# A seven-product Strassen scheme for the second MLP's down projection in a two-layer trunk

## The chip, the cores and the metric

The kernel runs on one core of one Trainium2 chip. Its time is the time of one execution in device microseconds (us), taken as the median of three runs, lower being better. Before the change it is 1189.18 us (1189.01 to 1190.25). The profile shows one execution of its own, taken by the hardware profiler; this document reads it by engine: PE (TensorE, matmuls), PEld (its loads of the stationary operand), DVE (VectorE), ACT (ScalarE), POOL (GpSimd) and SP (SyncE, which here only issues DMAs).

## The reference, cut to what matters

The trunk has two layers on 512 tokens of width 1024: a sparse-attention mixer with its MLP, then a convolution mixer with its MLP, and a last norm. The change lies in the second MLP, which is the last thing before that norm:

```python
def sq_relu_mlp(h, w1, w2):
    return jnp.square(jax.nn.relu(h @ w1)) @ w2

h = h + y
h = h + sq_relu_mlp(rmsnorm(h, norm_mlp_g[i]), mlp_w1[i], mlp_w2[i])
return rmsnorm(h, final_g)
```

`w1` is 1024 x 4096 and `w2` is 4096 x 1024, all in float32. Everything is computed to nearly float32 precision.

## The kernel before

**Three matmuls per product.** The engine multiplies numbers in a shorter float32 format (`F32R`). So each float32 operand is taken apart into a rounded part (hi) and a rest (lo), and a product is three matmuls: hi with hi, hi with lo, lo with hi (`mm3`, L90). For a weight this is `split` (L81): ACT copies the raw weight into `whi` (L86), then DVE subtracts to give `wlo` (L87). A unit of `split` here is 128 x 512 numbers, and units live in a ring of 12 buffers (`wsplit_mid`). Raw weights come as loads of 1 MB each, issued by SP, into a ring of two buffers (`wraw`).

**The second MLP** works in four groups g of 1024 hidden columns. In each group the up projection makes eight blocks j of hidden columns: 24 matmuls of 128 x 512 into a PSUM bank, then `hidden` inside `up_proj`: DVE does relu and the token scale (`hr`, L636), ACT squares it twice (`hf` in float32 at L638, `hh` as hi at L641), DVE subtracts for `hl` (L642). So each block has one trip from DVE to ACT and back. The first two blocks of group 0 (`ahead`) are computed early, at the end of the convolution's stage.

**The down projection** (L986 to L1014) takes each half of the 1024 output columns in turn. Four PSUM banks `dps`, one for each block b of 128 tokens, collect 8 k x 3 matmuls; the stationary operand is a 128 x 128 piece of `hh` or `hl`, the moving one a 128 x 512 weight unit. DVE then adds the bank to the result `y[b]` in SBUF (L1010). `y` starts as the transposed residual: 32 small transposes on PE into `rt` banks (L957) which ACT copies out (L958). In the last group `squares` and `finish` do the last norm (one `pow` on POOL for each block, L183) and store. The last half of the last group goes block by block of tokens, so that only one block's norm and store are left after the last matmul.

**Order.** A scheduler that simulates a timeline lays out each engine's queue when the program is built; at run time every engine goes through its own queue in order and waits on semaphores.

Of the kernel before, what the change touches and what calls it, by code (L numbers as in the profile page):

```python
# [18 lines left out]
P = 128  # L19
S = 512  # L20
D = 1024
KC = D // P
NB = S // P
# [19 lines left out]

ROW = 512
FILL = 64


@with_exitstack
def kernel(
# [7 lines left out]
    nc = tc.nc  # L57
# [42 lines left out]
    def bank(name="mm"):  # L100
        return acc.tile([P, S], F32, tag="mm", name=name)
# [57 lines left out]
    hT = [resid.tile([P, S], F32, name=f"hT{c}") for c in range(KC)]  # L159
# [469 lines left out]
    def up_proj(w, rr, pool, st=None, block=None, ahead=()):  # L629

        block = block or proj(w, g2)
        hid = []

        def hidden(ps):
            r = pool.tile([P, S], F32, tag="hr", name="hr", bufs=2)
            nc.vector.scalar_tensor_tensor(r, ps, 0.0, rr[0], op0=OP.max, op1=OP.mult)  # L636
            f = pool.tile([P, S], F32, tag="hf", name="hf", bufs=2)
            nc.scalar.activation(f, r, AF.Square)  # L638
            th = pool.tile([P, S], F32R, tag="hh", name="hh", bufs=10)
            tl = pool.tile([P, S], F32R, tag="hl", name="hl", bufs=10)  # L640
            nc.scalar.activation(th, r, AF.Square)  # L641
            nc.vector.tensor_sub(tl, f, th.bitcast(F32))  # L642
            hid.append((th, tl))

        done = 0
        if st is not None:
            first = list(ahead) or block([0])
            cols = rms_cols(st)
            first += block([1]) if len(first) < 2 else []
            rr[:] = [broadcast(cols, NB, bank("bc"))]  # L650
            for ps in first:
                hidden(ps)
            done = 2
        for j in range(done, KC):
            hidden(block([j])[0])
        return hid
# [11 lines left out]
            if k == 0:  # L668
                pw1.extend(ps)

    wsplit.append(ctx.enter_context(tc.tile_pool(name="wsplit_mid", bufs=12)))
    conv_ctx = ExitStack()
    late = conv_ctx.enter_context(tc.tile_pool(name="late", bufs=1))
    diags = [late.tile([P, max(TAPS0[c][0], TAPS1.get(c, (0, 0))[0]), 4, 32], F32, name=f"diag{c}")
# [53 lines left out]
            table(AF.Sigmoid, ghi[KC - 1].bitcast(F32))  # L728


    HS = S // 2
# [208 lines left out]
    conv_ctx.close()  # L940


    with tc.tile_pool(name="m2", bufs=1) as m2, \
            tc.tile_pool(name="m2_ps", bufs=2, space=PSUM) as m2_ps:
        fg = m2.tile([P, D], F32, name="fg")
        nc.scalar.dma_start(fg, final_g.rearrange("(o d) -> o d", o=1).to_broadcast([P, D]))
        y = [m2.tile([P, D], F32, name=f"y{b}") for b in range(NB)]
        ysq = small.tile([P, NB, 2], F32, name="ysq")
        fo = {}

        def residual():
            for b in range(NB):
                for half in range(2):
                    ps = m2_ps.tile([P, S], F32, tag="misc", name="rt")
                    for z in range(4):
                        c = 4 * half + z
                        nc.tensor.transpose(ps[:, z * P:(z + 1) * P], hT[c][:, b * P:(b + 1) * P], ident)  # L957
                    nc.scalar.activation(y[b][:, half * S:(half + 1) * S], ps, AF.Copy)  # L958

        def squares(b, half):  # L960

            hs = slice(half * S, (half + 1) * S)
            sq = tmp.tile([P, S], F32, tag="sq", name="sq")
            nc.scalar.activation(sq, y[b][:, hs], AF.Square, accum_out=ysq[:, b, half:half + 1])
            o = m2.tile([P, S], F32, tag=f"fo{half}", name="fo", bufs=3) if half else y[b][:, hs]
            nc.vector.tensor_mul(o, y[b][:, hs], fg[:, hs])
            fo[b, half] = o

        def finish(b):
            s1 = small.tile([P, 1], F32, tag="fs", name="fs", bufs=2)  # L970
            nc.vector.tensor_add(s1, ysq[:, b, 0:1], ysq[:, b, 1:2])
            r1 = inv_root(s1, 1, 1.0 / D, f"fr{b}")
            for half, eng in ((0, nc.sync), (1, nc.scalar)):
                o = fo[b, half]
                if half:
                    nc.vector.tensor_scalar(o, o, r1, None, op0=OP.mult)
                else:
                    nc.scalar.activation(o, o, AF.Copy, scale=r1)
                eng.dma_start(out[0, b * P:(b + 1) * P, half * S:(half + 1) * S], o)

        rr = []
        for g in range(NG):
            hid = up_proj(mlp_w1[1][:, g * D:(g + 1) * D], rr, m2, *((st, up, ahead) if g == 0 else ()))
            if g == 0:
                residual()
            w2 = mlp_w2[1][g * D:(g + 1) * D, :]  # L986
            for half in range(2):
                hs = slice(half * S, (half + 1) * S)
                last = g == NG - 1 and half == 1
                dps = [bank(f"dps{b}") for b in range(NB)]  # L990

                def mms(b, k, u):
                    tb = slice(b * P, (b + 1) * P)
                    mm3(dps[b], hid[k][0][:, tb], hid[k][1][:, tb], u[0][:, 0, :], u[1][:, 0, :],
                        k == 0, k == KC - 1)

                for k0 in (0, 4):
                    raw = load(w2, k0, 4, half * S, S)
                    units = []
                    for z in range(4):  # L1000
                        u = split(raw[:, z:z + 1, :])
                        units.append(u)
                        if not (last and k0):
                            for b in range(NB):
                                mms(b, k0 + z, u)
                for b in range(NB):
                    if last:
                        for z in range(4):
                            mms(b, 4 + z, units[z])
                    nc.vector.tensor_add(y[b][:, hs], dps[b], y[b][:, hs])  # L1010
                    if g == NG - 1:
                        squares(b, half)
                    if last:
                        finish(b)  # L1014


# [22 lines left out]
```

## Time and profile before

| What | us |
|---|---|
| Median of three runs | 1189.18 |
| The profiled execution's own time | 1186.75 |
| Its span (first to last instruction) | 1185.0 |
| PE busy in the span | 1150.8 |
| DVE busy | 663.3 |
| ACT busy | 498.2 |
| First matmul of the second MLP's first down projection | 873.1 |
| Last matmul of the program starts | 1177.75 |

A group of rows by line names the engine, the operation, the tiles written and read, the shape, the count, then the busy time in us and the mean of one in ns; behind the second bar stands how long the engine sat idle just before these instructions and who ended that. A row of a timeline gives start and duration in us; "x3" means three instructions merged, with the duration from the first start to the last end. Ends of matmuls are modelled, so how fast matmuls follow each other is read from their starts.

### The profile page before, as it was taken

The page shows a single profiled execution, that of the slowest core. Times are in us where ns is not written, and L with a number is a line of the kernel's source. Part 1 is how long each engine was busy: PE and PEld are TensorE (multiplying, and loading weights), DVE is VectorE, ACT ScalarE, POOL GpSimd, SP SyncE. Part 2 cuts the span into 40 slices and gives each one's busy share as a digit, 9 for nine tenths or more (in the row PEclk, how much of TensorE's full clock was granted, in tenths as well). Part 3 has the DMA queues.
Part 4 walks back from the last instruction along what each step waited for, and adds up shares of the span by engine and source line. Part 5 has one row for each costly group of instructions (what it writes and reads, how often), then busy time and mean ns, then how long its engine had stood idle before and what let it go on. Part 6 is the DMA issues. An engine that isn't in the chain of part 4 may idle for free.

```text
span 1185.0 us, 15284 instructions
## 1 busy us (share of the span) xinstructions
PE 1150.8 (97%) x5828; PEld 948.5 (80%) x5828; DVE 663.3 (56%) x1195; ACT 498.2 (42%) x936; POOL 247.5 (21%) x248
## 2 busy tenths in 40 slices
PE   7999999999999999999999988899999999999997
PEld 6778888877888888888888666689888888888886
DVE  4589854476434434434444998878544434434434
ACT  5353454545423423423435544466632432432422
POOL 2436643322005000000012667632100000000000
PEclk8999999999999999999999998999999999999999
DMA  6122222215233323322323563533322332332211
GB/s 229 36 71 72 89 84 77 71 36 182 78 100 107 98 80 107 107 83 78 125 71 116 151 172 91 161 108 115 117 86 92 107 107 72 106 107 92 86 36 71
DMA packets 104353, 117.84 MB, mean 99 GB/s; under 512 B 3817, under 2 KB 87609, under 8 KB 104280
## 3 DMA queue, kind: packets, MB, share of 16 engines
q1 hardware_dynamic: 102440, 112.89, 30.6%
q10 hardware_dynamic: 1840, 3.97, 0.9%
q8 instruction: 46, 0.75, 0.3%
q14 instruction: 27, 0.22, 0.1%
HBM read 112.56 MB, written 4.29 MB: 99 GB/s over the span
## 4 chain that ended last, share of the span: by engine, by line
PE 81%; DVE 12%; DMA 2%; issue 2%; ACT 1%; POOL 1%; SPq 0%; POOLq 0%; DVEq 0%; ACTq 0%
PE mm L91 19%; PE mm L93 19%; PE mm L92 19%; PE dps L93 5%; PE dps L92 5%; PE dps L91 5%; DVE score L482 2%; DVE m L480 2%; DVE conv L802 2%; DVE wlo L87 2%; DVE pa L798 1%; PE vps L91 1%; PE vps L92 1%; PE vps L93 1%; DMA xs<-in_x_dram 1%
## 5 line engine op out<-in xcount | busy, mean ns | idle before, releaser
L86 ACT ACTIVATE whi<-wraw 128x512 fp32r<-128x512 f32 x378 | 234.6, 631 | 469.9 <-PE mm L92 317.1
L92 PE MATMUL mm<-glo,whi 128*128 128x512 f32 (+1 forms) x928 | 337.0, 365 | 1.2 <-DVE glo L175 1.2
L93 PE MATMUL mm<-ghi,wlo 128*128 128x512 f32 (+1 forms) x928 | 337.1, 365 | 0.0
L91 PE MATMUL mm<-ghi,whi 128*128 128x512 f32 (+1 forms) x928 | 334.6, 366 | 1.9 <-ACT whi L86 0.8
L87 DVE TENSOR_TENSOR wlo<-wraw,whi 128x512 fp32r<-128x512 f32 x325 | 233.5, 726 | 177.7 <-ACT whi L86 174.1
L92 PEld LDWEIGHTS mm<-glo,whi 128*128 128x128 f32 x928 | 175.0, 189 | 31.0 <-issue 2.4
L91 PEld LDWEIGHTS mm<-ghi,whi 128*128 128x128 f32 x928 | 173.1, 189 | 32.6 <-issue 2.8
L93 PEld LDWEIGHTS mm<-ghi,wlo 128*128 128x128 f32 x928 | 175.0, 189 | 28.7 <-issue 1.1
L93 PE MATMUL mm<-hh,wlo 128*128 128x512 f32 x256 | 99.6, 389 | 0.0
L92 PE MATMUL mm<-hl,whi 128*128 128x512 f32 x256 | 99.6, 389 | 0.0
L92 PE MATMUL dps<-wlo,hh 128*128 128x512 f32 x256 | 99.6, 389 | 0.0
L91 PE MATMUL mm<-hh,whi 128*128 128x512 f32 x256 | 99.1, 389 | 0.0
L91 PE MATMUL dps<-whi,hh 128*128 128x512 f32 x256 | 99.1, 389 | 0.0
L93 PE MATMUL dps<-whi,hl 128*128 128x512 f32 x256 | 98.6, 389 | 0.0
L636 DVE SCALAR_TENSOR_TENSOR hr<-mm,rmsb 128x512 f32<-128x512 f32 x64 | 44.1, 691 | 91.9 <-PE mm L93 90.2
L87 POOL TENSOR_TENSOR wlo<-wraw,whi 128x512 fp32r<-128x512 f32 x53 | 70.9, 1342 | 89.6 <-ACT whi L86 89.5
L183 POOL TENSOR_TENSOR fr<-v,mhalf 128x1 f32<-128x1 f32 x4 | 2.2, 548 | 340.2 <-DVE v L181 340.2
L642 DVE TENSOR_TENSOR hl<-hf,hh 128x512 fp32r<-128x512 f32 x64 | 44.6, 697 | 41.9 <-ACT hh L641 41.9
L206 POOL TENSOR_TENSOR ss<-sq 128x512 f32<-128x512 f32 (+1 forms) x4 | 5.7, 1434 | 270.3 <-ACT sq L201 270.3
L790 POOL TENSOR_TENSOR pa<-pa,pt 128x512 f32<-128x512 f32 (+1 forms) x43 | 53.6, 1249 | 32.6 <-ACT pt L788 30.5
L92 PEld LDWEIGHTS mm<-hl,whi 128*128 128x128 f32 x256 | 48.0, 188 | 10.1
L92 PEld LDWEIGHTS dps<-wlo,hh 128*128 128x128 f32 x256 | 48.0, 188 | 10.0
(257 smaller groups left out, 1588.2 us busy)
## 6 DMA issues: line engine op xcount, KB each, us to landing
wraw<-in_mlp_w_dram SPq DMA_DIRECT2D x64, 1024.0 KB, 5.2
wraw<-in_conv_w_pw_dram SPq DMA_DIRECT2D x12, 1024.0 KB
wraw<-in_dsa_w_in_dram SPq DMA_DIRECT2D x10, 1024.0 KB, 9.1
wraw<-in_dsa_w_out_dram SPq DMA_DIRECT2D x4, 1024.0 KB, 4.9
sh<-flat SPq DMA_DIRECT2D x12, 260.0 KB, 3.6
sh<-flat SPq DMA_DIRECT2D x20, 138.0 KB, 2.8
xw<-in_dsa_w_in_dram ACTq DMA_DIRECT2D x4, 584.0 KB, 7.4
xs<-in_x_dram SPq DMA_DIRECT2D x4, 512.0 KB, 12.1
```

What stands on the lines that cost most here:

```text
L86: nc.scalar.activation(hi, src, AF.Copy)
L87: (eng or nc.vector).tensor_sub(lo, src, hi.bitcast(F32))
L91: nc.tensor.matmul(ps, wh, xh, start=start, stop=False)
L92: nc.tensor.matmul(ps, wh, xl, start=False, stop=False)
L93: nc.tensor.matmul(ps, wl, xh, start=False, stop=stop)
L480: nc.vector.max(m8s[-1], score[i])
L482: nc.vector.match_replace(score[i], m8s[i - 1], score[i], TAKEN)
L636: nc.vector.scalar_tensor_tensor(r, ps, 0.0, rr[0], op0=OP.max, op1=OP.mult)
L642: nc.vector.tensor_sub(tl, f, th.bitcast(F32))
L790: nc.gpsimd.tensor_add(pa, pa, pt)
L798: nc.vector.scalar_tensor_tensor(pa, sh(t), wt(t), pa, op0=OP.mult, op1=OP.add)
L802: nc.vector.scalar_tensor_tensor(cps, sh(t), wt(t), cps, op0=OP.mult, op1=OP.add)
```

## The change

The down projection of the second MLP is written anew. In a group, the 1024 hidden columns (k) are taken as even and odd blocks, the 512 tokens as two halves and the output columns as two halves. That is a 2 x 2 by 2 x 2 block product, which needs eight products of blocks when multiplied out; the new code forms seven (`p1`, `q5`, `q6`, `p2`, `p7`, `p3`, `p4`) from sums of blocks of weights and sums of blocks of hidden values. A product is 4 k x 2 token blocks x 3 = 24 matmuls of 128 x 512. Running sums stay in PSUM: `al` collects p1, q6, p7 and p4 in turn, `ga` q5 and p3, `be` p2. After each product DVE adds the two banks to two blocks of `y`, or subtracts them.

What else changes with it (line numbers of the kernel after):

- `hidden` (L1009) makes, for each pair of blocks j, seven operands of 256 tokens, in hi and lo: `b11`, `d1` from the even block, `b21`, `b22`, `e2`, `e3`, `e4` from the odd one. Sums go into the storage of `hT`, which is free by then. A pair has two trips from DVE to ACT and back in each block.
- Sums of weights (L1067, L1070, L1071, L1081) are DVE instructions of 128 x 2048, four in a group.
- The ring of split units has 8 buffers (`wsplit_m2`) in the place of 12, in storage of its own that opens when the old ring closes.
- The `rt` transposes stand ahead of the stage and have four PSUM banks; PE's order through the stage is the order of the code.
- In the last group two blocks of tokens end together in place of one.

```diff
-            w2 = mlp_w2[1][g * D:(g + 1) * D, :]
-            for half in range(2):
-                dps = [bank(f"dps{b}") for b in range(NB)]
...
-                for k0 in (0, 4):
-                    raw = load(w2, k0, 4, half * S, S)
...
-                    nc.vector.tensor_add(y[b][:, hs], dps[b], y[b][:, hs])
+        def parts(src, hi, lo):
+            nc.scalar.activation(hi, src, AF.Copy)
+            nc.vector.tensor_sub(lo, src, hi.bitcast(F32))
+
+        def hidden(j, ps):
...
+            nc.vector.scalar_tensor_tensor(r, ps, 0.0, rr[0], op0=OP.max, op1=OP.mult)
...
+                nc.scalar.activation(v[:, 0:3:2], r, AF.Square)
+                nc.vector.tensor_sub(v[:, 1], v[:, 0], v[:, 2])
+                parts(v[:, :2], xs[0][i], xs[1][i])
...
+                nc.scalar.activation(u[:, :2], r, AF.Square)
+                nc.vector.scalar_tensor_tensor(u[:, 2], u[:, 1], -1.0, v[:, 1], op0=OP.mult, op1=OP.subtract)
+                nc.vector.tensor_sub(u[:, 3], u[:, 1], v[:, 2])
+                nc.vector.scalar_tensor_tensor(u[:, 4], u[:, 2], -1.0, u[:, 0], op0=OP.mult, op1=OP.subtract)
+                parts(u, xs[2][i], xs[3][i])
+            a = {"a11": raw(0, 0), "a21": raw(1, 0), "a22": raw(1, 1, "wd")}
+            def product(bk, name, wn, xn, start):
+                for k in range(4):
+                    hi, lo = split(a[wn][:, k:k + 1, :])
+                    xh, xl = xop[xn, k]
+                    for z in range(2):
...
+                        for n, (l, m) in enumerate(((xh, hi), (xl, hi), (xh, lo))):
+                            nc.tensor.matmul(banks[bk, z], l[:, zs], m[:, 0, :], start=start and k == n == 0,
...
+            product("al", "p1", "a11", "b11", True)
+            to("al", 0, 0, OP.add)
+            s = a["s"] = m2.tile([P, 4, S], F32, tag="wd", name="ws", bufs=2)
+            nc.vector.tensor_add(s, a["a21"], a["a22"])
+            product("ga", "q5", "s", "d1", True)
+            to("ga", 1, 1, OP.subtract)
+            nc.vector.tensor_add(s, s, a["a11"])
+            nc.vector.tensor_add(a["a21"], a["a21"], a["a11"])
+            a["a12"] = raw(0, 1)
+            product("al", "q6", "s", "e2", False)
+            to("al", 1, 0, OP.add)
+            product("be", "p2", "a12", "b21", True)
...
+            product("al", "p7", "a21", "e3", False)
...
+            nc.vector.tensor_add(s, s, a["a12"])
+            product("ga", "p3", "s", "b22", False)
...
+            product("al", "p4", "a22", "e4", False)
```

Where the queues change. Until the last matmuls of the convolution's stage every engine has the same instructions in the same order and with the same waits as before. The first place is PE at the start of the stage: `rt` are the transposes of the residual, `bc` spreads the token scale over the partitions, `mm<-ghi` is the up projection's block j = 2. Before:

```order
L957 MATMUL rt<-ident,hT_102 128x128
L957 MATMUL rt<-ident,hT_103 128x128
L191 MATMUL bc<-diag,ones 128x128
L91 MATMUL mm<-ghi_104,whi 128x512
L92 MATMUL mm<-glo_112,whi 128x512
```

Now:

```order
L217 MATMUL rms_ps<-ones,ss 128x1 x2
L964 MATMUL rt<-ident,hT 128x128 x12
L193 MATMUL bc<-diag,ones 128x128 x2
L964 MATMUL rt<-ident,hT 128x128 x4
L193 MATMUL bc<-diag,ones 128x128 x2
L92 MATMUL mm<-ghi_97,whi 128x512
L93 MATMUL mm<-glo_105,whi 128x512
```

All transposes and all four `bc` now stand ahead of block j = 2; before, three `bc` and eight transposes came after it or in it. The second place is DVE in the up projection of a group, from the `hr` of one block to those that follow. Before:

```order
L636 SCALAR_TENSOR_TENSOR hr<-mm,rmsb 128x512
L87 TENSOR_TENSOR wlo<-wraw,whi 128x512
L642 TENSOR_TENSOR hl<-hf,hh 128x512
L87 TENSOR_TENSOR wlo<-wraw,whi 128x512
L636 SCALAR_TENSOR_TENSOR hr<-mm,rmsb 128x512
```

Now (`hT` is the borrowed storage for the sums, `xl` the lo parts, `ws` the sum of two raw weights):

```order
L88 TENSOR_TENSOR wlo<-wraw,whi 128x512
L1025 SCALAR_TENSOR_TENSOR hT<-hT 128x256
L1026 TENSOR_TENSOR hT<-hT 128x256
L1027 SCALAR_TENSOR_TENSOR hT<-hT 128x256
L88 TENSOR_TENSOR wlo<-wraw,whi 128x512
L1007 TENSOR_TENSOR xl_7750<-hT,xh_7746 128x1280
L1015 SCALAR_TENSOR_TENSOR hr<-mm,rmsb 128x512
L1067 TENSOR_TENSOR ws<-wraw 128x2048
L88 TENSOR_TENSOR wlo<-wraw,whi 128x512
L1020 TENSOR_TENSOR hT<-hT 128x256
L88 TENSOR_TENSOR wlo<-wraw,whi 128x512
L1071 TENSOR_TENSOR wraw<-wraw 128x2048
```

Sums that the down projection needs (L1067, L1071) now stand in DVE's queue inside the up projection, behind the `hr` of block 4 and ahead of that of block 5. The third place is SP's queue of loads for one group; `128x8x256` is a raw piece of `w1`, `128x4x512` one of `w2`:

```order
L77 DMA wraw<-in_mlp_w_dram 128x8x256 x2
L1034 DMA wraw<-in_mlp_w_dram 128x4x512
L77 DMA wraw<-in_mlp_w_dram 128x8x256 x2
L1034 DMA wraw<-in_mlp_w_dram 128x4x512 x3
L77 DMA wraw<-in_mlp_w_dram 128x8x256 x2
```

Eight loads of 1 MB for a group, as before, but one of `w2` (`a22`, into a buffer of its own) now goes ahead of the last two of `w1`; of the three that follow these, the first is `a11`, the second `a21`, the third `a12`.

## Rows read from the trace of the kernel before

**Rows 1.** The page's busy times, then its 40 slices of the span for PE, and for the granted clock of PE.

```profile
PE 1150.8 (97%) x5828; PEld 948.5 (80%) x5828; DVE 663.3 (56%) x1195; ACT 498.2 (42%) x936; POOL 247.5 (21%) x248
...
PE   7999999999999999999999988899999999999997
...
PEclk8999999999999999999999998999999999999999
```

**Rows 2.** Busy times by stage: the stretch, its length, then busy us of PE, PEld, DVE, ACT and POOL, the granted clock, the DMA engines' share and GB/s. The up projection of group 1, its down projection, and the whole from the first down projection's start to the last matmul.

```profile
916.60:960.20 43.60, 43.60 (x194) 36.09 (x193) 21.53 (x33) 18.23 (x30) 0.00 (x0) 1.00 0.29 97
960.20:1003.80 43.60, 43.60 (x194) 36.12 (x193) 15.71 (x24) 11.30 (x18) 0.00 (x0) 1.00 0.30 97
...
873.10:1178.00 304.90, 304.90 (x1346) 252.25 (x1344) 126.76 (x197) 99.27 (x167) 1.63 (x3) 1.00 0.26 86
```

**Rows 3.** All instructions on the tile `dps`: duration in ns (least, median, most), and the first and last start; the load of a stationary operand, its matmul, and the last matmul of the three.

```profile
L91 PEld LDWEIGHTS dps<-whi,hh x256: 187/188/188, 873.1 to 1177.1; 128*128 128x128 f32 x128
L91 PE MATMUL dps<-whi,hh x256: 389/389/389, 873.3 to 1177.3; 128*128 128x512 f32 x128
...
L93 PE MATMUL dps<-whi,hl x256: 388/389/389, 873.8 to 1177.7; 128*128 128x512 f32 x128
```

**Rows 4.** Groups of DVE's instructions from 850 us to the end, shapes kept apart.

```profile
L87 DVE TENSOR_TENSOR wlo<-wraw,whi 128x512 fp32r<-128x512 f32 x110 | 75.8, 689 | 93.6 <-ACT whi L86 93.6
L1010 DVE TENSOR_TENSOR y<-dps,y 128x512 f32<-128x512 f32 x32 | 20.9, 688 | 31.0 <-PE dps L93 31.0
L642 DVE TENSOR_TENSOR hl<-hf,hh 128x512 fp32r<-128x512 f32 x30 | 20.8, 693 | 20.5 <-ACT hh L641 20.5
L636 DVE SCALAR_TENSOR_TENSOR hr<-mm,rmsb 128x512 f32<-128x512 f32 x29 | 20.1, 692 | 44.9 <-PE mm L93 44.9
```

**Rows 5.** The same for the whole span, DVE's shapes of 256 elements and one row from a time when POOL is busy.

```profile
L860 DVE TENSOR_TENSOR u<-u,dr 128x256 f32<-128x256 f32 x16 | 6.7, 418 | 0.6 <-ACT dr L847 0.6
...
L900 DVE SCALAR_TENSOR_TENSOR hT<-mm,pv,hT 128x256 f32<-128x256 f32 x12 | 5.5, 479 | 6.2 <-PE mm L93 6.2
...
L817 DVE TENSOR_TENSOR u<-u,pilot 128x512 f32<-128x512 f32 x1 | 1.6, 1649 | 0.0
```

**Rows 6.** DVE in order of time: three instructions one behind the other, for the lo parts and for the adds to `y`.

```profile
818.96 1.89 DVE L87 TENSOR_TENSOR wlo<-wraw,whi 128x512 fp32r<-128x512 f32 x3
...
1154.37 2.05 DVE L1010 TENSOR_TENSOR y<-dps,y 128x512 f32<-128x512 f32 x3 [7.48 <-PE dps L93]
```

**Rows 7.** Groups of ACT's instructions, the first three from 850 us to the end, the last of the whole span.

```profile
L86 ACT ACTIVATE whi<-wraw 128x512 fp32r<-128x512 f32 x109 | 69.1, 634 | 183.4 <-PE dps L93 103.1 <-PE mm L92 77.2 <-ACT hh L641 2.0
L638 ACT ACTIVATE hf<-hr 128x512 f32<-128x512 f32 x29 | 18.4, 635 | 10.2 <-DVE hr L636 10.2
L641 ACT ACTIVATE hh<-hr 128x512 fp32r<-128x512 f32 x29 | 17.8, 615 | 0.0
...
L858 ACT ACTIVATE ghi<-u 128x256 fp32r<-128x256 f32 x16 | 6.7, 416 | 0.4
```

**Rows 8.** The start of the second MLP in order of time, on PE, POOL and DVE.

```profile
836.00 0.50 PE L215 MATMUL rms_ps<-ones,ss 128*128 128x1 f32 x4
...
836.78 1.53 POOL L183 TENSOR_TENSOR rms<-v,mhalf 128x4 f32<-128x4 f32 x1 [3.89 <-DVE v L181]
...
838.35 0.87 DVE L190 TENSOR_SCALAR diag<-ident,rms 128x128 f32<-128x128 f32 x4 [0.91 <-POOL rms L183]
...
838.93 0.47 PE L91 MATMUL mm<-ghi,whi 128*128 128x512 f32 x1
...
842.46 0.83 PE L191 MATMUL bc<-diag,ones 128*128 128x128 f32 x6
843.05 0.48 PE L91 MATMUL mm<-ghi,whi 128*128 128x512 f32 x1
...
845.22 1.03 PE L957 MATMUL rt<-ident,hT 128*128 128x128 f32 x8
846.01 0.47 PE L91 MATMUL mm<-ghi,whi 128*128 128x512 f32 x1
```

**Rows 9.** DMA issues by line: count, KB each, median us from issue to landing; the MLP's weights, and the four first loads of the program, which go out together.

```profile
wraw<-in_mlp_w_dram SPq DMA_DIRECT2D x64, 1024.0 KB, 5.2
...
xs<-in_x_dram SPq DMA_DIRECT2D x4, 512.0 KB, 12.1
```

**Rows 10.** The end of the program in order of time.

```profile
1177.75 0.39 PE L93 MATMUL dps<-whi,hl 128*128 128x512 f32 x1
...
1178.17 0.69 DVE L1010 TENSOR_TENSOR y<-dps,y 128x512 f32<-128x512 f32 x1 [0.78 <-PE dps L93]
...
1180.20 0.55 POOL L183 TENSOR_TENSOR fr<-v,mhalf 128x1 f32<-128x1 f32 x1 [2.18 <-DVE v L181]
1180.78 0.72 ACT L978 ACTIVATE y<-y,fr 128x512 f32<-128x512 f32 x1 [1.09 <-POOL fr L183]
```

More of the change, by code (lines that the diff above doesn't have):

```diff
@@ L157 @@
     cw = const.tile([P, 2 * P], F32, name="cw")[:, :KC * TAPS].rearrange("p (c t) -> p c t", t=TAPS)
-    hT = [resid.tile([P, S], F32, name=f"hT{c}") for c in range(KC)]
+    hT_all = resid.tile([P, KC, S], F32, name="hT")
+    hT = [hT_all[:, c] for c in range(KC)]
     ghi = [resid.tile([P, S], F32R, name=f"ghi{c}") for c in range(KC)]
@@ new lines @@
+        xs = [[m2.tile([P, n, HS], F32R, name=f"x{part}{n}{i}") for i in range(4)] for n in (2, 5)
+              for part in "hl"]
+        xop = {}
+        for i in range(4):
+            for z, name in enumerate(("b11", "d1")):
+                xop[name, i] = xs[0][i][:, z], xs[1][i][:, z]
+            for z, name in enumerate(("b21", "b22", "e2", "e3", "e4")):
+                xop[name, i] = xs[2][i][:, z], xs[3][i][:, z]
+        free = hT_all.rearrange("p c (h t) -> p (c h) t", h=2)
+        def parts(src, hi, lo):
+            nc.scalar.activation(hi, src, AF.Copy)
+            nc.vector.tensor_sub(lo, src, hi.bitcast(F32))
@@ new lines, in down_strassen, with raw, to, complete @@
+        def down_strassen(w, last):
+            def raw(r, k, tag=None):
+                t = (m2 if tag else wraw).tile([P, 4, S], F32, tag=tag or "wraw", name="wraw",
+                                               bufs=2)
+                nc.sync.dma_start(t, rows(w)[:, k:KC:2, r * S:(r + 1) * S])
+                return t
+            a = {"a11": raw(0, 0), "a21": raw(1, 0), "a22": raw(1, 1, "wd")}
+            banks = {}
+            def product(bk, name, wn, xn, start):
[3 more added lines that the diff above has]
+                    for z in range(2):
+                        if (bk, z) not in banks:
+                            banks[bk, z] = bank(bk) if bk == "al" else dbank(bk)
+                        zs = slice(z * P, (z + 1) * P)
+                        for n, (l, m) in enumerate(((xh, hi), (xl, hi), (xh, lo))):
+                            nc.tensor.matmul(banks[bk, z], l[:, zs], m[:, 0, :], start=start and k == n == 0,
+                                             stop=k == 3 and n == 2, skip_group_check=not start)
+            def to(bk, t, half, op):
+                for z in range(2):
+                    b = 2 * t + z
+                    o = y[b][:, half * S:(half + 1) * S]
+                    nc.vector.tensor_tensor(o, o, banks[bk, z], op=op)
+            def complete(t, half):
+                if last:
+                    for z in range(2):
+                        squares(2 * t + z, half)
+            product("al", "p1", "a11", "b11", True)
[10 more added lines that the diff above has]
+            product("be", "p2", "a12", "b21", True)
+            to("be", 0, 0, OP.add)
+            complete(0, 0)
+            product("al", "p7", "a21", "e3", False)
+            to("al", 1, 1, OP.subtract)
+            complete(1, 1)
+            nc.vector.tensor_add(s, s, a["a12"])
+            product("ga", "p3", "s", "b22", False)
+            to("ga", 1, 0, OP.add)
+            complete(1, 0)
+            if last:
+                for z in range(2):
+                    finish(2 + z)
+            product("al", "p4", "a22", "e4", False)
+            to("al", 0, 1, OP.subtract)
+            complete(0, 1)
+            if last:
+                for z in range(2):
+                    finish(z)
@@ new lines @@
+        rr = []
+        with tc.manual_schedule(engines={PE}):
+            for g in range(NG):
+                if g == 0:
+                    rr.append(broadcast(rms_cols(st), NB, bank("bc")))
+                    for j in range(2):
+                        hidden(j, ahead[j])
+                else:
+                    up = proj(mlp_w1[1][:, g * D:(g + 1) * D], g2)
+                for j in range(0 if g else 2, KC):
+                    hidden(j, up([j])[0])
+                down_strassen(mlp_w2[1][g * D:(g + 1) * D, :], g == NG - 1)
```

67 lines of the change are left out of this document (27 added, 40 removed).

## The prediction

> **What bounds the kernel now.** I read the busy times first: PE is busy in 97% of the span and in nearly every slice, at full granted clock [rows 1]. Then I went to the stage of the change, since a mean over the span says nothing of it. From the first down projection to the last matmul, 304.9 us, PE never stands still; DVE works 126.8 us of that and ACT 99.3, POOL almost nothing [rows 2]. In the two halves of a group DVE has 21.5 of 43.6 us and 15.7 of 43.6. Third, the pace: the modelled duration of a matmul is 389 ns, but between the first starts at 873.3 and 1177.3 lie 1341 matmuls (768 of `dps` and 576 of three up projections, less the last three), so one starts every 0.2267 us [rows 3]. Hence 24 matmuls take 5.44 us and a group of 384 takes 87.1. Here PE is the bound: DVE and ACT sit idle before their instructions until PE or each other lets them go [rows 4, 7]. A matmul taken away is worth its pace as long as DVE can follow.
>
> **What goes.** A group's down projection has 7 x 24 = 168 matmuls in place of 192. Four groups lose 96, and 96 x 0.2267 = 21.8 us. The program's order confirms the counts, so that the change might not do what it says needs no case of its own. The operand shapes are those of before, so I take the pace as kept. The nearest row for a smaller worth is the load of the stationary operand, 0.188 us [rows 3]: if that set the pace, 96 x 0.188 = 18.0.
>
> A rule of the Trainium skill is weighed here. The rows show one matmul of 512 columns every 227 ns, 1341 times in a row. The Trainium skill, page "TensorE: Matmul & The Clock Gate", section "Back-to-back issue gap", puts the sustained pace of such load-and-matmul pairs at about 131 ns at full clock. By that page the saving would be an estimated 96 x 0.131 = 12.6 us, the rest of the spacing being something else that stays. The trace does not agree with 131 ns, and the measurement decides.
>
> **What DVE gets.** Prices: 512 elements 0.69 us [rows 4]; 256 elements 0.42 for a plain and 0.48 for a scalar-tensor form [rows 5]. So an element costs (0.689 - 0.418) / 256 = 1.06 ns, and by that 1280 elements cost 1.50 us and 2048 cost 2.32, both estimates. One behind the other, three of 512 take 1.89 us, so each after the first costs 0.60; three adds from PSUM take 2.05 [rows 6]. A busy POOL makes such an instruction 1.65 us [rows 5], but POOL has nothing to do in this stage [rows 2]. A group now has 44 lo parts (16 of `w1`, 28 of `w2` or its sums; 30.4), 14 adds (9.7), 8 `hr` (5.5), 16 of 256 (7.2), 4 `xl` of 512 (2.8), 4 of 1280 (6.0) and 4 sums of weights (9.3): 70.9 us standing apart, about 64 in succession, beside PE's 360 x 0.2267 = 81.6. Before it was about 37 beside 87. ACT gets 44 copies (27.9), 8 squares (5.1), 4 copies of 512 (2.5) and 4 of 1280 (1.21 each by the same slope, 4.9) [rows 7], 40 us beside 81.6. So on the sums nobody overtakes PE, but DVE goes from 43% to between 78% and 87%, and it takes its queue in order.
>
> What counts is when PE waits for DVE. The tightest place is the start of `p7`: it adds into bank `al`, and the two adds of `q6` must have read that bank first. In DVE's queue they stand behind the sums, the splits of `p2` and three splits of `p7`. From the `hr` of block 0 up to them DVE has 47.3 us in succession, 52.8 apart; PE has 264 matmuls, 59.8 us. That is 7 us of slack in groups 1 to 3, and I cost them at nothing.
>
> **Group 0** has less. The block j = 2 began at 838.93; three `bc` (0.59) and eight transposes (0.79) that came later now come first [rows 8], which shifts work but adds none: 840.3. The new chain has eight more transposes ahead of `rms_ps`, then `pow` (1.53) and `diag` (0.87) as before, ending at 839.2 + 0.8 = 840.0, and two last `bc`: 840.5. Cost 0.2 us, between 0 and 1. Then DVE splits blocks 2 and 3 (4 x 0.60, until 842.4); only then is a raw buffer free for the last two blocks of `w1`, whose load lands 5.2 us later [rows 9] at 847.6, and after ACT's copy DVE goes on at 848.3. From there to the adds of `q6` stand 63 DVE instructions, those two among them (23 lo parts, 6 `hr`, 16 of 256, 4 `xl` of 512, 4 of 1280, 4 sums, 6 adds): 44.4 us in succession, 49.4 apart. So they end between 892.7 and 897.7. `p7` is due 240 matmuls after 840.4, at 894.8. DVE is 2.1 us early or 2.9 late. A late DVE finds its inputs ready and runs in succession, so I take a point nearer to that end: 1 us of PE waiting, from 0 to 2.9.
>
> The rest I cost at nothing with its cover: the new sums depend on loads of the same bytes as before at 30% of the DMA engines [rows 2]; the smaller ring of 8 units still lets DVE be 8 units ahead, four blocks of the up projection or two products, 10.9 us of PE. If that cover went, a late unit would show as PE waiting for `wlo` or `whi`.
>
> **The tail.** Before, from the last matmul's start at 1177.75 one block is left, and the last scale ends at 1180.78 + 0.72 [rows 10]. Now two blocks end within three matmuls. The second one's `pow` (0.55) and scale on ACT (0.72) queue behind the first one's: 1.3 us more, between 0.7 (part of it overlaps) and 2.
>
> **Sum.** -21.8 + 0.2 + 1.0 + 1.3 = -19.3 us. On the profiled execution: span 1185.0 - 19.3 = 1165.7, and 1.75 us around it give 1167.4 in place of 1186.75. The median shown is 2.43 us above that execution, so I predict 1169.9. With every term at its good end (-21.8 + 0 + 0 + 0.7) it is 1168.1; at its bad end (-21.8 + 1 + 2.9 + 2) 1173.3. Within 0.2% (2.4 us) I could not tell a difference from none.
>
> **Rivals.**
>
> First, DVE's trips to ACT. `hidden` has 16 in a group now, 8 before. Before, DVE stood idle 20.5 us before 30 `hl`, 0.68 each, with a split already put between [rows 4]. If each new trip costs DVE half of that, 0.34, group 0 is late by 2.9 + 14 x 0.34 = 7.7 and the others (52.8 + 5.4 against 59.8) are not: -21.8 + 0.2 + 7.7 + 1.3 = -12.6, so 1176.6. For it: two trips in a row in each block and a strict order. Against it: DVE has more to do in between, and a DVE that is late does not find ACT late.
>
> Second, the slower side, by the same mechanism at full strength: each trip costs DVE x us wherever it stands, late or not, with durations apart. PE then waits 2.9 + 14x in group 0 and 16x - 7 in each of three groups, 62x - 18.1 in all. From x = 0.62 the gain of 20.3 is gone; at the measured 0.68 it is 24.1, which gives 1193.0, slower. Against it stands that the row's 0.68 comes from a DVE with nothing else to do.
>
> Third, the load of `a21`. DVE's first sum (L1067) needs it, it takes the buffer of the last `w1` piece, and everything in DVE's queue (splits of `a11`, sums, `hr` of block 5) stands behind. That buffer is free about 1.4 us after the `hr` of block 3, and DVE has 13.7 us of work in succession from the sum to the last `xl` that `p1` needs; PE gives 4 blocks and 18 matmuls, 25.9. So a landing up to about 10.8 us costs nothing. At 5.2 it is free; at the 12.1 of crowded loads [rows 9] it is 1.3 in each of four groups, 1175.1.
>
> Fourth, a removed matmul is worth only its 0.188 us load: -18.0 + 2.5, so 1173.7. Against it: with 0.188 of load in each 0.227, PEld is busy 83% and not all the time [rows 2]. The Trainium skill's page named above would make it still less; its own figure gives 1179.1.
>
> **How the numbers follow.** The forecast has 0.62 (1168 to 1173.3), trips at half price 0.20 (1174 to 1180), a late `a21` 0.04, the load's pace 0.03, trips at full price 0.11, of which 0.07 slower by over 0.2% and 0.04 within it. So faster 0.89, same 0.04, slower 0.07. The range from 1167 to 1180 holds the first four and leaves the last out.
>
> **What would show it.** Right: 0.2267 us between matmuls through products too; a down projection of 38.1 us in groups 1 to 3, with no idle time of PE; in group 0 at most a wait at `p7` for an add of DVE (L1057); DVE busy 64 to 71 us in a group; from the last matmul's start to the last scale 5.0 us in place of 3.75; instructions ahead of 829 us unchanged. Wrong: waits of PE for `wlo`, `xl` or an add in every group (the trips), DVE idle at L1067 for a DMA (`a21`), sums of 2048 elements far above 2.3 us, or another pace.

## The result and the profile after

The kernel after takes 1167.57 us (median of four runs, 1166.11 to 1169.90), the kernel before beside it 1189.1. The ratio is 0.982 (95% interval 0.980 to 0.984). Later runs on another chip give 1167.63 beside 1188.15, so 20.5 us less. The forecast was 1169.9, in a range from 1167 to 1180.

The execution that the profiler took is the slowest of the four: 1169.90 us, with a span of 1168.1. Its busy times and slices, to be read beside [rows 1]:

```profile
PE 1130.7 (97%) x5732; PEld 932.3 (80%) x5732; DVE 773.2 (66%) x1347; ACT 535.1 (46%) x984; POOL 245.4 (21%) x248
...
PE   7999999999999999999999998989999999999997
```

PE has 96 matmuls fewer (5732 for 5828) and is as full as before; DVE has 110 us more work. Stage by stage, in the columns of [rows 2]: the up projection of group 1, the down projections of groups 0 and 1, and part of that of group 3.

```profile
911.22:955.00 43.78, 43.78 (x195) 36.26 (x194) 31.48 (x47) 20.35 (x30) 0.00 (x0) 1.00 0.29 96
873.00:911.20 38.20, 38.20 (x171) 31.61 (x170) 34.24 (x51) 20.42 (x32) 0.00 (x0) 1.00 0.33 111
955.00:993.00 38.00, 38.00 (x169) 31.46 (x168) 33.39 (x49) 18.84 (x30) 0.00 (x0) 1.00 0.33 111
...
1118.10:1156.00 37.90, 37.90 (x169) 31.36 (x168) 33.85 (x51) 19.90 (x38) 0.00 (x0) 1.00 0.09 29
```

PE is busy in every microsecond of these stretches, at full clock, though DVE now works 31.5 + 33.4 = 64.9 us in a group. The pace is read from the tile `al`, in the columns of [rows 3]:

```profile
L1049 PE MATMUL al<-whi,xh x128: 389/389/389, 876.5 to 1158.7; 128*128 128x512 f32 x128
...
L1049 PE MATMUL al<-wlo,xh x128: 388/389/389, 877.0 to 1159.2; 128*128 128x512 f32 x128
```

From 876.5 to 1159.2 lie 672 matmuls of products and 576 of three up projections, 1247 intervals: 0.2267 us each, the pace of before. The start of the stage, in the order of [rows 8] (`rms_ps` has two runs of four matmuls; the first one's row before stands below it):

```profile
832.26 0.50 PE L217 MATMUL rms_ps<-ones,ss 128*128 128x1 f32 x4
...
840.20 0.50 PE L217 MATMUL rms_ps<-ones,ss 128*128 128x1 f32 x4
840.74 1.64 PE L964 MATMUL rt<-ident,hT 128*128 128x128 f32 x12
...
843.73 0.47 PE L92 MATMUL mm<-ghi,whi 128*128 128x512 f32 x1
```

```profile
828.94 0.50 PE L215 MATMUL rms_ps<-ones,ss 128*128 128x1 f32 x4
```

The end of the program, to be held against [rows 10] (two blocks of tokens now end together):

```profile
1158.90 1.36 DVE L1057 TENSOR_TENSOR y<-y,al 128x512 f32<-128x512 f32 x2 [0.68 <-PE al L1049]
...
1159.15 0.39 PE L1049 MATMUL al<-wlo,xh 128*128 128x512 f32 x1
1159.68 0.63 ACT L971 ACTIVATE sq<-y 128x512 f32<-128x512 f32 x1 [1.17 <-DVE y L1057]
...
1160.43 0.69 DVE L973 TENSOR_TENSOR y<-y,fg 128x512 f32<-128x512 f32 x1 [0.17 <-ACT sq L971]
...
1162.02 1.09 POOL L185 TENSOR_TENSOR fr<-v,mhalf 128x1 f32<-128x1 f32 x2 [4.32 <-DVE v L183]
...
1163.22 0.71 ACT L985 ACTIVATE y<-y,fr 128x512 f32<-128x512 f32 x1
```

**Where the 20 us are.** The instructions ahead of the stage are those of before, in the same order, yet in this execution the first `rms_ps` of the stage starts at 832.26 us, where it started at 828.94 before; over the thirteen profiled executions of this document, which share this part, it lies anywhere from 828.9 to 832.7. That spread is not the change's. So the stage is measured by itself:

| Stretch | before | after | difference |
|---|---|---|---|
| first `rms_ps` to block j = 2 | 9.99 | 11.47 | +1.48 |
| block j = 2 to the last matmul's start | 338.82 | 315.42 | -23.40 |
| last matmul's start to the end of the span | 7.25 | 8.95 | +1.70 |
| sum | 356.06 | 335.84 | -20.22 |

Of the first two rows, 1.38 us is only shifted (three `bc` and eight transposes that now come ahead of block j = 2, [rows 8]). What is left is +0.10 and -22.0, where 96 x 0.2267 is 21.8.

### The profile page after: what moved, and what is told of

Same layout as the page of the kernel before. It is cut to its first block, busy times and chain, and to the rows that moved or that the text cites. A ratio compares the mean times of both kernels' runs of the same rounds, so it can differ in the third digit from the quotient of the medians.

```text
span 1168.1 us, 15341 instructions
## 1 busy us (share of the span) xinstructions
PE 1130.7 (97%) x5732; PEld 932.3 (80%) x5732; DVE 773.2 (66%) x1347; ACT 535.1 (46%) x984; POOL 245.4 (21%) x248
## 4 chain that ended last, share of the span: by engine, by line
PE 85%; DVE 8%; DMA 2%; issue 2%; ACT 1%; POOL 0%; SPq 0%; ACTq 0%; DVEq 0%
PE mm L92 21%; PE mm L93 20%; PE mm L94 20%; PE al L1049 7%; PE ga L1049 4%; DVE wlo L88 2%; PE be L1049 2%; DVE conv L804 2%; DVE pa L800 2%; PE vps L92 1%; PE vps L93 1%; PE vps L94 1%; DMA xs<-in_x_dram 1%; DMA wraw<-in_dsa_w_in_dram 1%; PE lg L93 1%
## 5 line engine op out<-in xcount | busy, mean ns | idle before, releaser
L94 PEld LDWEIGHTS mm<-hh,wlo 128*128 128x128 f32 x256 | 48.1, 188 | 10.0
L92 PEld LDWEIGHTS mm<-hh,whi 128*128 128x128 f32 x256 | 48.1, 188 | 10.0
L93 PEld LDWEIGHTS mm<-hl,whi 128*128 128x128 f32 x256 | 48.1, 188 | 9.9
L638 DVE SCALAR_TENSOR_TENSOR hr<-mm,rmsb 128x512 f32<-128x512 f32 x32 | 22.0, 691 | 46.4 <-PE mm L94 45.6
L1049 PE MATMUL al<-whi,xh 128*128 128x512 f32 x128 | 49.8, 389 | 0.0
L1049 PE MATMUL al<-whi,xl 128*128 128x512 f32 x128 | 49.8, 389 | 0.0
L1049 PE MATMUL al<-wlo,xh 128*128 128x512 f32 x128 | 49.8, 389 | 0.0
```

Of the source, the lines that this page charges most:

```text
L1049: nc.tensor.matmul(banks[bk, z], l[:, zs], m[:, 0, :], start=start and k == n == 0, stop=k == 3 and n == 2, skip_group_check=not start)
```

## The experiments

**Eight products in the new frame.** Is it the count of matmuls, or something else that the new code brought?

```diff
-                nc.scalar.activation(v[:, 0:3:2], r, AF.Square)
-                nc.vector.tensor_sub(v[:, 1], v[:, 0], v[:, 2])
+                nc.scalar.activation(v[:, :2], r, AF.Square)
...
-                parts(u, xs[2][i], xs[3][i])
+                parts(u[:, :2], xs[2][i][:, :2], xs[3][i][:, :2])
...
+            for bk, xe, xo, wa, wb, t, half in (
+                    ("al", "b11", "b21", "a11", "a12", 0, 0), ("ga", "d1", "b22", "a11", "a12", 1, 0),
+                    ("be", "b11", "b21", "a21", "a22", 0, 1), ("al", "d1", "b22", "a21", "a22", 1, 1)):
...
+                product(bk, wa, wa, xe, True)
+                product(bk, wb, wb, xo, False)
+                to(bk, t, half, OP.add)
```

> The new frame (order of PE by the code, adds product by product, raw pieces of w2 by k parity, ring of 8) with the plain scheme: eight products of 24 matmuls in a group, no sums of weights or of hidden values. My theory: the gain is the count of matmuls times the pace and nothing else, so 96 matmuls x 0.2267 = 21.8 us come back: 1167.6 + 21.8 = about 1189.4, the level of the kernel before (1189.1), with PE never idle and a last-matmul-to-end of about 9 us as in the kernel after. Rival: the gain is the frame's (order, banks, smaller ring, early transposes), then it stays near 1168 to 1175.

Measured: 1189.86 us, ratio to the kernel before 1.0014 (1.0004 to 1.0024). PE does not wait anywhere in the stage:

```profile
841.91 0.47 PE L92 MATMUL mm<-ghi,whi 128*128 128x512 f32 x1
...
1179.09 0.39 PE L1045 MATMUL al<-wlo,xh 128*128 128x512 f32 x1
```

From block j = 2 to the last matmul's start are 337.18 us, against 315.42 in the kernel after: 21.76 more, and 96 x 0.2267 is 21.76. From there to the end at 1188.0 are 8.9 us. So all of the gain has gone (by the medians +22.3 us), and what is left against the kernel before is about the longer tail. The frame gains nothing; the eighth product left out is the whole of it.

**How much room DVE has.** The two runs repeat a subtraction (once, and three times) whose result does not change.

```diff
                 parts(u, xs[2][i], xs[3][i])
+                for _ in range(1):
+                    nc.vector.tensor_sub(xs[3][i], u, xs[2][i].bitcast(F32))
```

> One more xl subtraction of 1280 elements for each pair of blocks, four in a group, 4 x 1.49 = 6.0 us of DVE; the result does not change. My theory (DVE runs its queue in succession and its trips to ACT cost next to nothing): in group 0, where DVE's adds of q6 ended 2.1 us ahead of p7, PE now waits 6.0 - 2.1 = 3.9 us, at p7 or shortly ahead of it; in groups 1 to 3 the slack of 7 us or more takes it, no wait. So +3.9 us, about 1171.5. Rival (each of the 16 trips of a group costs DVE half of 0.68 us): groups 1 to 3 have 59.8 - 52.8 - 5.4 = 1.6 us left and wait 4.4 us each, so +17, about 1185.

> The same with three more of these subtractions for each pair, 17.9 us of DVE in a group. My theory: group 0 is late by 17.9 - 2.1 = 15.8 us; groups 1 to 3 need 47.3 + 17.9 = 65.2 us from the hr of block 0 to the adds of q6 where PE gives 59.8, so PE waits about 5.4 us in each (up to 7.5 where DVE does not run in full succession): +32 to +38, about 1200 to 1206. DVE is then the bound through the up projections. Rival (DVE's total alone decides, 65 + 17.9 = 83 beside 81.6 us in a group, and the place in the queue does not matter): +1.4 us in each group, about 1173.

Measured: 1191.71 us, +24.1, where my theory said +3.9; and with three repeats 1240.78 us, +73, where it said +32 to +38. Both are far off: the first lies nearer to its rival (+17), the second beyond both (its rival said 1173). In the second, PE waits 50.9 us for `xl` and `xh` in `p1` and `q6`, and slow matmuls stand behind these waits. The waits of PE in the first run, and around one of them DVE and then PE in order of time:

```profile
PE al L1051 <- DVE xl L1030: 17.1, 4, 7.2
```

```profile
975.11 1.48 DVE L1007 TENSOR_TENSOR xl<-hT,xh 128x1280 fp32r<-128x1280 f32 x1
976.51 1.27 DVE L1059 TENSOR_TENSOR y<-y,ga 128x512 f32<-128x512 f32 x2
977.71 2.28 DVE L1083 TENSOR_TENSOR ws<-ws,wraw 128x2048 f32<-128x2048 f32 x1
979.91 1.89 DVE L88 TENSOR_TENSOR wlo<-wraw,whi 128x512 fp32r<-128x512 f32 x3
981.71 1.48 DVE L1030 TENSOR_TENSOR xl<-hT,xh 128x1280 fp32r<-128x1280 f32 x1
```

```profile
983.25 0.80 PE L1051 MATMUL al<-whi,xl 128*128 128x512 f32 x1 [3.30 <-DVE xl L1030]
983.84 0.63 PE L1051 MATMUL al<-wlo,xh 128*128 128x512 f32 x1
984.27 0.63 PE L1051 MATMUL al<-whi,xh 128*128 128x512 f32 x1
```

Two things are to be seen. The wait is not at `p7`. It is at `q6`, at its fourth block (behind 19 of its matmuls), which needs the `xl` of the last pair of hidden blocks; and the repeat of that `xl` stands in DVE's queue 5.1 us behind the first one, behind two adds, a sum of 2048 and three splits. And behind the wait the matmuls start 0.43 us apart in place of 0.2267. Added up over the trace: the four gaps are 17.75 us longer than the pace, and 34 slow matmuls after them cost another 6.9, together 24.7. So over a quarter of the price is not the wait itself.

That left open whether DVE's load or the place of the repeat had cost this. The next run has the same instructions on DVE in the same order through the stage, but writes where nobody reads:

```diff
                 parts(u, xs[2][i], xs[3][i])
+                nc.vector.tensor_sub(u, u, xs[2][i].bitcast(F32))
```

> The same 6.0 us of DVE in a group as in the run with one more xl subtraction (four instructions of 128x1280), but now they write to storage that nobody reads, so that nothing waits for them. My theory after that run: its waits in groups 1 to 3 came from the place of the repeated subtraction in DVE's queue (behind a sum of 2048 and three splits, while q6's fourth block needs it), not from DVE's load. So groups 1 to 3 have no wait now (there the first xl of the last pair ended 3.2 us early); group 0 keeps one of about 4.6 us at q6, with about 1.5 us of half pace behind it: +6, about 1174. Rival (DVE's load as such is paid, 6.0 us in every group): +24 again, about 1191.

Measured: 1174.78 us, +7.2. One wait of PE, in group 0, and none in the other three:

```profile
PE al L1050 <- DVE xl L1007: 4.6, 1, 4.6
```

```profile
896.94 0.79 PE L1050 MATMUL al<-whi,xl 128*128 128x512 f32 x1 [4.64 <-DVE xl L1007]
```

In group 1 the extra instruction starts at 982.67, behind the same sum and splits as above (there 981.71), and PE does not wait for it. So 6 us more of DVE in a group are free in groups 1 to 3, and what the earlier run paid there was an operand made late. They only just fit, and the place that fills up is `p7`, whose bank the adds of `q6` must have read first. In group 1 the first add (half of this x2) ends at 987.15:

```profile
986.48 1.27 DVE L1058 TENSOR_TENSOR y<-y,al 128x512 f32<-128x512 f32 x2
```

```profile
987.30 0.47 PE L1050 MATMUL al<-whi,xh 128*128 128x512 f32 x1
```

That is 0.15 us of room, and 0.16 in groups 2 and 3. In the kernel after it is 3.4 us in group 1: the adds start at 975.82, the first ends at 976.50, and `p7` starts at 979.86.

```profile
975.82 1.27 DVE L1057 TENSOR_TENSOR y<-y,al 128x512 f32<-128x512 f32 x2
```

The wait in group 0 is one of place too. The scheduler laid DVE's queue anew for both runs, and it put the last `xl` of group 0 behind a sum of 2048, two adds and five splits that follow it in the kernel after. First the run with dead work, then the kernel after, here with the same `xl` of group 1:

```profile
893.21 2.28 DVE L1082 TENSOR_TENSOR ws<-ws,wraw 128x2048 f32<-128x2048 f32 x1
895.41 1.48 DVE L1007 TENSOR_TENSOR xl<-hT,xh 128x1280 fp32r<-128x1280 f32 x1
```

```profile
885.73 1.49 DVE L1007 TENSOR_TENSOR xl<-hT,xh 128x1280 fp32r<-128x1280 f32 x1
887.13 2.29 DVE L1081 TENSOR_TENSOR ws<-ws,wraw 128x2048 f32<-128x2048 f32 x1
...
965.84 1.49 DVE L1007 TENSOR_TENSOR xl<-hT,xh 128x1280 fp32r<-128x1280 f32 x1
```

In the kernel after, this `xl` of group 0 ends at 887.22 and PE reads it at 891.69, 4.5 us later. In group 1 it ends at 967.33; `p1` begins at 958.10 and the reader is 67 matmuls behind, at 973.29: 6.0 us. Of the extra work only three subtractions stand ahead of it in group 0, an estimated 4.2 us in succession (1.40 each), which 4.5 us would just have held; the sum, adds and splits that were put ahead of it are another 6.4. No run has the extra work in the old order.

**The order of the products.** `p7` straight behind `q6`, `p2` behind it:

```diff
+            product("al", "p7", "a21", "e3", False)
+            to("al", 1, 1, OP.subtract)
+            complete(1, 1)
             product("be", "p2", "a12", "b21", True)
             to("be", 0, 0, OP.add)
             complete(0, 0)
-            product("al", "p7", "a21", "e3", False)
-            to("al", 1, 1, OP.subtract)
-            complete(1, 1)
```

> p7 comes straight behind q6 and p2 behind p7, so that bank al is added into twice in a row and DVE's two adds of q6 stand between. My theory: PE waits at each of the four places, in groups 1 to 3 from 0.3 us (adds that start as soon as the bank is done) to 2.1 us (adds behind four splits, as they stood in the kernel after), in group 0 about 3 us; with up to 1.5 us of half pace behind each wait: +2 to +15, about 1176 as a middle. Rival (the adds are in time wherever p7 stands, so the order of the products carries nothing): no change, 1167.6.

Measured: 1178.59 us, +11.0. PE waits in each group for the adds of `q6`:

```profile
PE al L1049 <- DVE y L1057: 7.6, 4, 2.5
```

That is 2.5 us in group 0 and 1.70 in each of the others; with the slow matmuls after the first of them, the stretch from block j = 2 to the last matmul is 10.3 us longer than in the kernel after. The product on another bank that stands between `q6` and `p7` hides all of this.

**The ring of split units.**

```diff
-    with tc.tile_pool(name="wsplit_m2", bufs=8) as ws2, \
+    with tc.tile_pool(name="wsplit_m2", bufs=4) as ws2, \
```

> The ring of split units has 4 buffers in place of 8. My theory (the ring gives DVE its lead: 8 units are two products or four blocks, 4 are 5.4 us of PE in the products): ACT's copies now wait for PE to free a unit, ACT's copies of hidden values stand behind them, and the margin of 2 us in group 0 and 3 to 6 us in the others is used up: PE waits in the products, some us in a group, +4 to +20. Rival (the ring's size does not matter as long as a unit or two are ready): no change, 1167.6.

Measured: 1182.70 us, +15.1. From block j = 2 to the last matmul the trace has 13.3 us more. In each group PE waits 1.74 us for DVE at the first unit of `q6`:

```profile
PE al L1049 <- DVE wlo L88: 7.0, 4, 1.7
```

That unit is split from the sum of weights that L1070 makes, and between the sum and its split DVE's queue has an `xl` of 1280 and two adds (group 1):

```profile
968.25 0.68 DVE L88 TENSOR_TENSOR wlo<-ws,whi 128x512 fp32r<-128x512 f32 x1
968.96 2.29 DVE L1070 TENSOR_TENSOR ws<-ws,wraw 128x2048 f32<-128x2048 f32 x1
971.17 1.49 DVE L1007 TENSOR_TENSOR xl<-hT,xh 128x1280 fp32r<-128x1280 f32 x1
972.58 1.27 DVE L1057 TENSOR_TENSOR y<-y,ga 128x512 f32<-128x512 f32 x2
973.77 1.89 DVE L88 TENSOR_TENSOR wlo<-ws,whi 128x512 fp32r<-128x512 f32 x3
```

From the last split of `q5` to the first of `q6` lie 5.5 us, as long as PE needs for the four units of a product (5.44). With 8 buffers this first unit is ready 3.8 us before PE reads it in group 0 and 5.9 us in the others; with 4 DVE cannot get far enough ahead.

**The load of `a21`,** issued twice:

```diff
-                nc.sync.dma_start(t, rows(w)[:, k:KC:2, r * S:(r + 1) * S])
+                for _ in range(2 if (r, k) == (1, 0) else 1):
+                    nc.sync.dma_start(t, rows(w)[:, k:KC:2, r * S:(r + 1) * S])
```

> The load of a21 is issued twice into the same buffer, so that the sums that need it can start only when the second has landed, some 5 us later than before; the scheduler puts DVE's sums behind one more xl and one more split. My theory: DVE's queue has room for it in groups 1 to 3 (the last xl for q6 was 6.0 us early there), and in group 0 4.5 us; no wait in groups 1 to 3, up to 1 us in group 0, with half pace behind it: 0 to +2.5, about 1168.5. Rival (what the prediction called the load of a21: the sums hold up everything behind them): 5 us in each group, +20, about 1188.

Measured: 1167.70 us, no change; from block j = 2 to the last matmul's start are 315.42 us, as in the kernel after. The first sum of group 0 starts 9.2 us ahead of `p1`, where it was 14.2 there, so the load is late by 5 us. DVE waits for the load, PE for nothing:

```profile
L1068 DVE TENSOR_TENSOR ws<-wraw 128x2048 f32<-128x2048 f32 x4 | 9.2, 2293 | 7.0 <-DMA wraw<-in_mlp_w_dram 7.0
```

It uses up room, though: the first add of `q6` ends 1.1 us before `p7` in group 0, where the kernel after has 2.8.

**The tail.** First the last product by blocks of tokens, then also the second half's product with the norm's weight in other storage:

```diff
+                apart = last and name == "p4"
+                for k in range(4):
+                    units[k] = split(a[wn][:, k:k + 1, :])
+                    for z in range(1 if apart else 2):
+                        mms(k, z)
+                if apart:
+                    for k in range(4):
+                        mms(k, 1)
```

> In the last product of the program (p4 of group 3) the 12 matmuls of the first token block come ahead of the 12 of the second, so that one block ends 2.7 us earlier and only one block's norm and store are left behind the last matmul; its adds, squares, norm and store are written block by block. My theory (the second block queued behind the first is the whole of the longer tail): the time from the last matmul's start to the end of the span goes from 8.9 back to about 7.25 us, so -1.65 us. Rival (the longer tail is in the stores or in their engines, whatever the order): it stays at 8.9. The whole time, with a spread of some us from run to run, can hardly tell; the tail is read from the trace.

```diff
-            o = y[b][:, hs]
-            nc.vector.tensor_mul(o, o, fg[:, hs])
+            o = hT[b] if half else y[b][:, hs]
+            nc.vector.tensor_mul(o, y[b][:, hs], fg[:, hs])
```

> The last product by token blocks, as in the run before, and in addition the product of y and the norm's weight for the second half of the columns goes to storage of its own (hT, free by then), so that it need not wait until ACT has squared the same y, as it does where it is written in place. My theory: the longer tail has three parts, two blocks at once, the stores, and this wait, which pushes DVE's sum of squares (L978) back by about 0.6 us; so from the last matmul's start to the end of the span 8.1 goes to 7.3 to 7.6, and the last scale ends 4.0 to 4.2 us behind the last matmul's start in place of 4.7. Rival (ACT's scale of the block before sets the chain): 8.1 and 4.7 stay.

Measured, from the last matmul's start: to the end of the last scale, then from there to the end of the span, and the sum.

| Kernel | last scale | stores | sum |
|---|---|---|---|
| before | 3.75 | 3.50 | 7.25 |
| after | 4.78 | 4.17 | 8.95 |
| last product by blocks | 4.68 | 3.43 | 8.11 |
| and the product elsewhere | 3.79 | 3.46 | 7.25 |

The first edit gives half of what was expected, and nearly all of it in the stores; the second gives the rest, more than expected. Its mechanism stands in the rows of the end above: L973 multiplies `y` in place, so it may not start before ACT has read the same `y` (the 0.17 put down to `sq`), and the sum of squares that the norm waits for (L978) is queued behind its 0.69. With the first edit alone L978 starts 0.64 us behind the end of ACT's square, with both 0.03. That is 0.61 of the 0.89 us by which the second edit brings the last scale forward; the other 0.28 is ACT, which is free that much earlier because it is done with the scale of the block before, so the rival had a share. The kernel before wrote that half to a tile of its own. What the second edit would give without the first wasn't tried. In time the first version (1167.98 us) cannot be told from the kernel after; the second had 1166.60. It was run again beside the kernel after:

> The kernel after, unchanged, beside the next one on the same chip, so that the tail's 1.7 us can be told from the spread of some us between runs: about 1167.6.

> The version with the last product by token blocks and the second half's product in storage of its own, again, in more rounds beside the kernel after: by its trace it is 1.7 us shorter behind the last matmul and the same ahead of it, so 1.7 us below the kernel after, about 1165.9. Rival (its 1.0 us below the median of the kernel after was the spread of runs): equal.

Measured: 1167.63 us for the kernel after (ratio 0.9827, 0.9814 to 0.9841) and 1166.34 for this version (0.9820, 0.9806 to 0.9834). In the traces the tail is 8.94 and 7.26 us. So the 1.7 us are seen where they should be, but the intervals overlap: by time alone it is not shown to be faster than the kernel after. Against the kernel before it is the lowest of the versions.

## Why the prediction was right, step by step

**The removed matmuls: right.** 96 at 0.2267 us, 21.8, against 22.0 in the stage; eight products in the same frame bring them back. The rival that a matmul is worth only the load of its stationary operand, 0.188 us, would have given 18.0. It falls in the same trace too, at a place where matmuls have 256 columns and each has a load of its own:

```profile
819.91 0.28 PE L93 MATMUL pw<-glo,whi 128*128 128x256 f32 x1
820.03 0.28 PE L94 MATMUL pw<-ghi,wlo 128*128 128x256 f32 x1
...
819.91 0.19 PEld L94 LDWEIGHTS pw<-ghi,wlo 128*128 128x128 f32 x1
820.03 0.19 PEld L93 LDWEIGHTS mm<-glo,whi 128*128 128x128 f32 x1
```

They start 0.12 us apart, closer than a load lasts, so the load's duration is no floor; at 512 columns the pace is 0.107 us longer. The 131 ns of the Trainium skill (page "TensorE: Matmul & The Clock Gate", section "Back-to-back issue gap") do not hold for these matmuls of 512 columns: the stage gave 22.0 us for 96 of them, not 12.6.

**DVE's load: right.** 64.9 us in a group against 64 to 71, at the succession end. Sums of 2048 took 2.28 to 2.29 us (estimated 2.32), the `xl` of 1280 1.49 (1.50); ACT's copies of 1280 took 1.26 (1.21).

**The wait at `p7` in group 0: the place was right, the cost too high.** Forecast 1.0 us, between 0 and 2.9; PE did not wait at all:

```profile
894.75 1.28 DVE L1057 TENSOR_TENSOR y<-y,al 128x512 f32<-128x512 f32 x2
```

The adds end at 896.03, `p7` is due 96 matmuls behind `p1`, at 898.2: 2.2 us early, where the succession end of the forecast said 2.1. From 851.25, where DVE goes on with the last two blocks' splits, it needed 44.8 us, and the succession sum was 44.4; the chosen point nearer to that end should have been the end itself. "The tightest place is the start of `p7`" held: the first of the two adds ends 2.8 us before `p7` in group 0 and 3.4 to 3.7 in the others, and no other operand or bank of a product is ready with less room (the last `xl` for `p1` 3.1 us ahead in group 0 and 4.7 in the others, for `q6` 4.5 and 6.0). That PE stops at `q6` and not at `p7` in runs with more work for DVE comes from the place that the `xl` got in their queues.

**Groups 1 to 3 at nothing: right,** with half the slack that was forecast, 3.4 to 3.7 us in place of 7. From the `hr` of block 0 to the adds of `q6` DVE is busy 48.1 us in group 1 (forecast 47.3 in succession), but it also stands idle 8.8 us there, between its instructions, and the sums of durations had no term for that. The dead work fits with 0.15 us to spare. The first two rivals, DVE's trips to ACT, cost PE nothing: before the `xl` DVE sat idle for ACT 4.2 and 2.1 us in all four groups, 0.2 us for each of 32.

```profile
L1007 DVE TENSOR_TENSOR xl<-hT,xh 128x1280 fp32r<-128x1280 f32 x16 | 23.8, 1490 | 4.2 <-ACT xh L1006 4.2
...
L1007 DVE TENSOR_TENSOR xl<-hT,xh 128x512 fp32r<-128x512 f32 x16 | 11.0, 687 | 2.4 <-ACT xh L1006 2.1
...
L1067 DVE TENSOR_TENSOR ws<-wraw 128x2048 f32<-128x2048 f32 x4 | 9.1, 2286 | 0.6 <-DMA wraw<-in_mlp_w_dram 0.6
```

The third, a late `a21`, cost DVE 0.6 us here and, when forced, 7.0, and PE nothing: the claim that a later landing is free held, with a sum 5 us later and the queue that the scheduler laid for it.

**The covers: right.** Eight units in the ring are enough and four are too few; no run shows a size between.

**The start: right,** +0.1 against +0.2. **The tail: sized too small,** 1.70 against 1.3, and only in part for the reason given. Of the 1.3 charged, the second block's `pow` is there (two take 1.09 us in place of 0.55), but its scale adds only 0.08, since it overlaps. Not priced were 0.42 us between the last matmul and the first `pow` (2.87 in place of 2.45) and 0.67 in the stores. Both edits of the tail together take all 1.7 back: most of the part in the stores goes with the order by blocks, and the rest when the product with the norm's weight is no longer written in place. That it is written in place is a part of the change that its description leaves out and that I did not price.

**The sum.** -21.8 + 0.2 + 1.0 + 1.3 = -19.3 was forecast, -20.2 found in the stage. The misses cancel in part: 1.0 too much at `p7`, 0.2 too little for the matmuls and 0.1 too much at the start, against 0.4 too little for the tail. The forecast median lay 2.3 us too high: 0.9 is this difference, and the other 1.4 lie in the 2.43 us by which I lifted the profiled execution to the median, a spread between runs that later runs of the kernel before did not repeat in full (1188.15 in place of 1189.18). The measured time stands only 0.6 us above the low end of the range, which held it narrowly.

## What to carry to other kernels

Where one engine is full through a stage and nobody waits, work taken off it is worth its pace, and work put on an idler engine is free up to a margin that is found operand by operand: take each product's last input, and the last reader of each bank that it writes, and compare when they are done with when the product needs them. That margin is spent by an instruction's place in its queue as much as by its length. Where a result is accumulated in several steps, a product on another bank between two on the same one hides the adds.

## What had not been expected of the hardware

A stop of PE can cost more than it lasts. In the run with one repeated subtraction, three of the four waits (7.2, 3.30 and 3.30 us) have six to twelve matmuls behind them that start 0.43 us apart, about half as fast; so has the 4.64 us of the run with dead work, and soon behind it the 2.5 us of the run with another order. The granted clock there is 0.50, that is 1.2 of 2.4 GHz (the run with dead work: during the wait and behind it, then a stretch further on, in the columns of [rows 2]):

```profile
891.90:896.90 5.00, 0.40 (x2) 0.00 (x0) 5.00 (x6) 0.63 (x1) 0.00 (x0) 0.74 0.05 13
896.90:901.00 4.10, 4.06 (x10) 3.19 (x11) 4.10 (x6) 0.63 (x1) 0.00 (x0) 0.50 0.73 240
902.00:907.00 5.00, 5.00 (x24) 4.12 (x23) 3.44 (x6) 2.05 (x5) 0.00 (x0) 1.00 0.66 210
```

That is some 2 us on top of such a wait (6.9 us in all in the run with one repeated subtraction, 2.3 for this one). But behind the fourth wait of the run with one repeated subtraction, 3.30 us in group 3, the pace is full at once. Behind waits of 1.70 us in the run with another order the pace was full at once, three times of three; with the ring of 4, two of four waits of 1.74 us had a slow stretch behind them and two had not. So a wait of 1.7 to 3.3 us may or may not have this price here, and what decides it these runs do not show.
